# Three weight tiles of a decoder layer's mixer, laid 64 bytes lower in SBUF

## The chip, the cores and the metric

One core of a Trainium2 chip. The metric is the device time of one execution in microseconds (us), the median of the runs shown. The shorthand of the profile: PE is TensorE's matmul stream and PEld its weight loads, DVE is VectorE, ACT is ScalarE, POOL is GpSimd, SP is SyncE (here only a DMA queue).

## The reference, cut to what matters

One decoder layer on 512 tokens of width 1024, in float32: a half-step SwiGLU FFN, a mixer, and a second half-step FFN, each between a norm before and a norm after.

```
x = x + 0.5 * PostNorm_a(SwiGLU_1(PreNorm_a(x)))
x = x +       PostNorm_b(W_out [HGRN2_heads(h) ; mLSTM_heads(h)]),  h = PreNorm_b(x)
x = x + 0.5 * PostNorm_c(SwiGLU_2(PreNorm_c(x)))
```

All that matters here is the front of the mixer. It reads one combined projection of the normed input, cut into column groups of 512 (and a few gate columns):

```
hq, hf, hi, hgate, mq, mk, mv, mo, mig, mfg = split_cols(h @ w_in, SPLIT_SIZES)
forget = lbh + (1.0 - lbh) * sigmoid(hf)                     # HGRN2's forget gate
... silu(hq) ...                                             # HGRN2's queries
qk = silu(causal_depthwise_conv(concat([mq, mk]), conv_w, conv_b))   # mLSTM's q and k
```

Three of these groups, hf, hq and (mq, mk), are wanted with features on the partitions and tokens along the free axis; the others (hi, mv, hgate, mo) with tokens on the partitions.

## The kernel before, in words

**Numbers.** Every float32 matrix is split into a high part (ACT casts it to fp32r, line 283) and a low part (DVE subtracts the high one from the raw values, line 285). A product is three fp32r matmuls: high by high, high by low, low by high. A weight tile holds both parts one behind the other: 2 x 1024 floats for each partition, 8 KB.

**The weights' ring.** All weight tiles lie in one long SBUF tile, `w` (line 270): 96 floats of room in front, four places of 2048 floats, 128 floats of room behind. `split` (line 260) takes the next tile of a list made beforehand, asks `lie` (line 248) for a free place and a shift within it, and issues the cast and the subtraction. `LIES` (line 98) gives the shifts in floats for each kind of tile. For a tile that isn't "out" and isn't a 512-wide mixer tile (kind "any") it is 0 in all cases that matter here. The 512-wide tiles of the mixer (kind "mix") lie 16 floats (64 bytes) lower.

**The three projections.** Each of hf, hq and (mq, mk) has four weight tiles of 128 columns (`f` in `mix_items`), split and used in this order, and they take the places 0, 1, 3, 2 of the ring. The tile is the stationary operand, the transposed activations are the moving one: four tiles `xq0` to `xq3`, each of half of the features and half of the tokens (256), high and low part one behind the other.
- hf goes first. `head_mm` (line 543, matmuls on line 548) does the first 256 tokens while the first FFN's last rows are still being normed: 24 matmuls for a tile (8 slices of the features by 3 products). `forget_gates` then has `in_mm` do the other 256 tokens (`in_k`, line 534, matmuls on line 538): again 24 for a tile.
- hq and the convolution's (mq, mk) are jobs (`job_f`), 48 matmuls on line 538 for a tile, that the mixer's code pulls forward with `fill` between its own small matmuls. After the first (mq, mk) tile has begun come HGRN2's small matmuls (lines 1368, 1373, 1419), and after the fourth the gate rows (line 1466). After them come the token-major projections (lines 187 to 189, `mm3`), in which the 512-wide weight tile is the moving operand and the activations are the stationary one.

**The FFN products.** Line 608, in `prod`, is the FFNs' big group, with the same shape as lines 538 and 548: 128x128 weights and 256 moving columns, 24 matmuls for a product, 8 for each of the three pairs of parts. One layout detail is needed below. In the FFNs, tile `xq0` is viewed as `x0` (line 139), whose low part begins 16 floats (64 bytes) further on than in the other three. It is read by the middle eight matmuls of products p1, c1 and c3.

**Addresses in SBUF,** from the built program, in bytes within a partition: `w` begins at 87136, and its place 0 with the shift 0 at 87136 + 96 x 4 = 87520. `xq1`, `xq2`, `xq3`, `xq0` begin at 33440, 41632, 49824, 58016. Within a tile the slices of the features lie 512 bytes apart in the weights and 1024 bytes apart in the activations, and places lie 8192 bytes apart, so that start addresses modulo 512 stay the same through a tile.

Of the kernel before, what the change touches and what calls it, by code (L numbers as in the profile page):

```python
# [22 lines left out]
RAW, WBUF, PAD, LATE, NEXT, FRONT, STEP = 3, 4, 128, 112, 64, 96, 16  # L23
# [71 lines left out]

FREE = (2, 3, 0, 1)
FREE2 = (3, 2, 0, 1)
LIES = {"any": (0, -16, -80, 48), "mix": (-16, 0, -80, 48), "out": (-80, 48, 0, -16)}


class Load:
# [17 lines left out]
class Layer:  # L119
# [128 lines left out]
    def lie(self, kind):  # L248

        used = [o for _, o, _ in self.slot.values()]  # L250
        at = LIES[kind]

        first = 1 + (kind == "out")
        tries = [(n, d) for n in self.free for d in (at[:first] if n < 2 else at[first - 1 :: -1])]
        for n, d in tries + [(n, d) for d in at[first:] for n in self.free]:
            o = FRONT + 2 * D * n + d
            if o + 2 * D <= self.wt.shape[1] and all(abs(o - a) >= 2 * D for a in used):
                return n, o

    def split(self):  # L260

        nc = self.nc
        it = self.items.popleft()
        raw = self.raw[it.key]
        _, a, b = raw.shape
        if it.dst:
            w = it.dst()
        else:
            if self.wt is None:
                self.wt = self.wp.tile([P, 2 * D * WBUF + FRONT + PAD], F32R, name="w")  # L270
            if not self.slot and it.key[0] != "mix":
                self.free = deque(FREE2 if it.key[0] == "f2" else FREE)
            n, o = self.lie("out" if it.key[1] == "out" else "mix" if it.key[0] == "mix" and b == 512 else "any")
            self.free.remove(n)
            w = self.wt[:, o : o + 2 * D].rearrange("p (b k t) -> p b k t", b=2, k=a)
            self.slot[id(w)] = n, o, w
        hi, lo = self.both(w)
        if it.sums:
            raw, hi, lo = (self.flat(v)[:, QUARTER:] for v in (raw, hi, lo))
        self.ready.append((w, it.dst is not None))  # L280
        rows = it.rows
        if rows is None:
            nc.scalar.copy(hi, raw)  # L283
            yield
            self.low = nc.vector.tensor_tensor(lo, raw, hi.bitcast(F32), op=ALU.subtract)  # L285
        else:
            for j in range(a):
                nc.scalar.activation(hi[:, j], raw[:, j], AF.Copy, scale=rows[:, j : j + 1])
            yield
            for j in range(a):  # L290
                nc.vector.scalar_tensor_tensor(
                    lo[:, j], raw[:, j], rows[:, j : j + 1], hi[:, j].bitcast(F32), op0=ALU.mult, op1=ALU.subtract
                )
        with self.behind(*self.hold):
            for out, other in it.adds:
                o, c = self.raw[out], self.raw[other]

                late = out[1] >= (HEAD if out[0] == "f1" else 1)
                added = (nc.vector if late else nc.gpsimd).tensor_tensor(o, o, c, op=ALU.add)  # L299
                if not late:  # L300
                    self.pooled = added
        self.load_due(self.done)
        self.done += 1
        yield
# [410 lines left out]
    def start(self, norm, xn):  # L715
# [8 lines left out]
        split = self.split()  # L724
        step(q[1][0], q[1][1])
        next(split)
        step(q[1][0])
        next(split)
        step(q[0][0], q[1][0])
        head = deque(HEADS)  # L730
# [1170 lines left out]
```

## Time and profile before

| what | value |
|---|---|
| runs, us | 934.08, 934.02, 931.58; median 934.02 |
| the profiled execution's own time, us | 933.69 |
| its span on the core, us | 932.0 (1.69 lie around it) |
| granted TensorE clock | 0.998 of full speed |
| busy share of the span | PE 99%, DVE 82%, ACT 56%, POOL 20% |
| stages in the span, us | first FFN 0 to 342; hf, hq and convolution's projections with HGRN2's first matmuls 342 to 424; rest of the mixer to 603; second FFN to the end |

How to read it: the profile has a row for each group of instructions, with its count, its busy time and the mean length of one. A matmul's length is from its start to its modelled end, and matmuls are pipelined, so lengths overlap. What a stream of them costs is the pitch, the time from one start to the next. Where a row tells of one unbroken stretch, the pitch is its length less one matmul, over its count less one.

### The profile page before, as it was taken

To read this page: it belongs to the slowest core of one execution; us is meant where nothing else is said; L and a number is where in the kernel's file an instruction comes from. 1 tells how busy PE (TensorE), PEld (TensorE's weight loads), DVE (VectorE), ACT (ScalarE), POOL (GpSimd) and SP (SyncE) were. 2 spreads that over 40 slices of the span, in tenths; PEclk is the share of its full clock that TensorE was granted. 3 is DMA by queue.
4 is the path that set the end of the run, shared out by engine and by line. 5 is a ranking of instruction groups with operands and counts; after the bars stand their busy time and mean duration, and the time that the engine had idled before them with its cause. 6 is when DMAs were issued, how large, how long until landed. Compare 5 with 4: busy or idle time off the path is not lost.

```text
span 932.0 us, 18308 instructions
## 1 busy us (share of the span) xinstructions
PE 921.7 (99%) x7423; PEld 887.4 (95%) x7423; DVE 765.9 (82%) x992; ACT 525.2 (56%) x757; POOL 186.9 (20%) x256
## 2 busy tenths in 40 slices
PE   8999999999999999999999999999999999999997
PEld 7999999999999999998887888899999999999997
DVE  5899978889888776698847564799898989998886
ACT  6645455557565466956633444495454545756661
POOL 3531112121111045452321210304000000011002
PEclk9999999999999999999999999999999999999999
DMA  9245679776797925798742124452453435279542
GB/s 310 76 138 157 181 182 214 195 157 142 209 273 238 262 65 150 151 184 208 152 98 69 46 72 132 137 162 66 135 159 123 136 111 174 84 221 261 165 153 91
DMA packets 118766, 145.42 MB, mean 156 GB/s; under 512 B 7413, under 2 KB 91417, under 8 KB 118682
## 3 DMA queue, kind: packets, MB, share of 16 engines
q1 hardware_dynamic: 102714, 129.05, 44.2%
q0 software_dynamic: 15680, 14.69, 11.6%
q8 instruction: 58, 0.95, 0.4%
q10 hardware_dynamic: 288, 0.52, 0.2%
q14 instruction: 26, 0.21, 0.1%
HBM read 142.14 MB, written 31.46 MB: 186 GB/s over the span
## 4 chain that ended last, share of the span: by engine, by line
PE 62%; ACT 1%; DVE 0%; issue 0%; POOL 0%; DVEq 0%; POOLq 0%; ACTq 0%
PE ps L608 22%; PE ps L955 8%; PE ps L538 6%; PE ps L187 5%; PE ps L189 5%; PE ps L188 5%; PE ps L947 4%; PE ps L1373 2%; PE ps L353 1%; PE ps L548 1%; PE ps L1466 0%; PE ps L1671 0%; PE ps L1644 0%; PE ps L1419 0%; PE ps L1668 0%; PE ps L1431 0%
## 5 line engine op out<-in xcount | busy, mean ns | idle before, releaser
L283 ACT CAST w<-raw 128x1024 fp32r<-128x1024 f32 x246 | 251.3, 1028 | 199.0 <-PE ps L608 93.6
L285 DVE TENSOR_TENSOR w<-raw,w 128x1024 fp32r<-128x1024 f32 x246 | 298.9, 1219 | 30.9 <-ACT w L283 29.5
L608 PE MATMUL ps<-xq,w 128*128 128x256 f32 x2016 | 237.1, 277 | 0.0
L608 PEld LDWEIGHTS ps<-xq,w 128*128 128x128 f32 x2016 | 232.9, 188 | 0.0
L608 PE MATMUL ps<-sq,w 128*128 128x256 f32 x1512 | 178.0, 276 | 0.3
L608 PEld LDWEIGHTS ps<-sq,w 128*128 128x128 f32 x1512 | 174.2, 188 | 1.0 <-ACT ps L659 0.9
L299 DVE TENSOR_TENSOR raw<-raw,raw 128x1024 f32<-128x1024 f32 x72 | 89.8, 1251 | 7.8 <-DMA raw<-in_ffn_w_in_dram 6.1
L955 PE MATMUL ps<-w,hs 128*128 128x256 f32 x672 | 81.0, 276 | 0.0
L947 PE MATMUL ps<-w,hs 128*128 128x256 f32 x672 | 79.2, 276 | 0.0
L955 PEld LDWEIGHTS ps<-w,hs 128*128 128x128 f32 x672 | 78.4, 188 | 0.0
L187 PE MATMUL ps<-w,xq 128*128 128x512 f32 x192 | 77.9, 407 | 0.1
L947 PEld LDWEIGHTS ps<-w,hs 128*128 128x128 f32 x672 | 77.5, 188 | 0.0
L189 PE MATMUL ps<-w,xq 128*128 128x512 f32 x192 | 74.8, 391 | 0.0
L188 PE MATMUL ps<-w,xq 128*128 128x512 f32 x192 | 74.8, 390 | 0.0
L538 PE MATMUL ps<-xq,w 128*128 128x256 f32 x480 | 57.5, 282 | 0.0
L538 PEld LDWEIGHTS ps<-xq,w 128*128 128x128 f32 x480 | 56.6, 189 | 0.5 <-issue 0.5
L887 POOL DMA_DIRECT2D f2sums<-in_ffn_w_out_dram x15 | 20.0, 1482 | 176.9 <-DMA f2sums<-in_ffn_w_out_dram 176.9
L827 ACT CAST hs<-hf 128x1024 fp32r<-128x1024 f32 x32 | 33.7, 1053 | 28.8 <-PE ps L955 21.1
L828 DVE TENSOR_TENSOR hs<-hf,hs 128x1024 fp32r<-128x1024 f32 x32 | 39.1, 1221 | 8.7 <-ACT hs L827 8.2
L887 POOL DMA_DIRECT2D f1sums<-f1sums x26 | 23.2, 892 | 105.9 <-DMA f1sums<-in_ffn_w_out_dram 53.0
L187 PEld LDWEIGHTS ps<-w,xq 128*128 128x128 f32 x192 | 36.1, 188 | 8.5 <-issue 1.0
L189 PEld LDWEIGHTS ps<-w,xq 128*128 128x128 f32 x192 | 36.1, 188 | 8.1 <-DVE xq L360 0.3
(262 smaller groups left out, 1223.3 us busy)
## 6 DMA issues: line engine op xcount, KB each, us to landing
raw<-in_ffn_w_in_dram SPq DMA_DIRECT2D x98, 512.0 KB, 5.3
raw<-in_ffn_w_out_dram SPq DMA_DIRECT2D x44, 512.0 KB, 4.5
raw<-in_w_mix_in_dram SPq DMA_DIRECT2D x28, 512.0 KB, 3.6
raw<-f2sums SPq DMA_DIRECT2D x15, 512.0 KB, 5.6
raw<-f1sums SPq DMA_DIRECT2D x13, 512.0 KB, 7.6
raw<-in_w_mix_out_dram SPq DMA_DIRECT2D x8, 512.0 KB, 3.7
f2sums<-in_ffn_w_out_dram SPq DMA_DIRECT2D x30, 128.0 KB, 5.9
f2sums<-in_ffn_w_out_dram SPq DMA_DIRECT2D x15, 256.0 KB, 5.7
```

Of the source, the lines that this page charges most:

```text
L187: mm(ps, sh, mh, start=start, stop=False, **kw)
L188: mm(ps, sh, ml, start=False, stop=False, **kw)
L189: mm(ps, sl, mh, start=False, stop=stop, **kw)
L283: nc.scalar.copy(hi, raw)
L285: self.low = nc.vector.tensor_tensor(lo, raw, hi.bitcast(F32), op=ALU.subtract)
L299: added = (nc.vector if late else nc.gpsimd).tensor_tensor(o, o, c, op=ALU.add)
L538: mm(ps[:, u0:u1], w[:, a, k, :], self.xop(k, b, u0, u1), start=k + n + m == 0, stop=k == ND - 1 and n == 2, skip_group_check=True,)
L608: self.nc.tensor.matmul(ps[:, c], wb[b][:, k, v], left[d][:, k, :], start=first and a + n + k == 0, stop=n == 2 and k == KH - 1, skip_grou ...
L828: self.nc.vector.tensor_tensor(lo, src, hi.bitcast(F32), op=ALU.subtract)
L887: nc.gpsimd.dma_start(to[:, a:b], v, accum_op=ALU.add)
L947: mm(out, a[kk][:, i * P : (i + 1) * P], w[:, b, kk, QUARTER * v : QUARTER * (v + 1)], start=begin and c == kk == n == 0, stop=kk == 1 and ...
L955: mm(ps[:, QUARTER * c : QUARTER * (c + 1)], A[a][:, c], B[b], start=begin and c == n == 0, stop=n == 2, skip_group_check=True,)
```

## The change

`lie` gets a kind "low", that returns place 0 and a shift of -16 floats, with no search. `split` asks for it for a mixer tile that isn't 512 wide, whenever place 0 is free. With the order of places above, this holds for the first tile of each of the three projections, and for no other tile.

```
-LIES = {"any": (0, -16, -80, 48), "mix": (-16, 0, -80, 48), "out": (-80, 48, 0, -16)}
+LIES = {"any": (0, -16, -80, 48), "mix": (-16, 0, -80, 48), "low": (-16,), "out": (-80, 48, 0, -16)}
...
         first = 1 + (kind == "out")
+        if kind == "low":
+            return 0, FRONT + at[0]
         tries = [(n, d) for n in self.free for d in (at[:first] if n < 2 else at[first - 1 :: -1])]
...
-            n, o = self.lie("out" if it.key[1] == "out" else "mix" if it.key[0] == "mix" and b == 512 else "any")
+            mix = "mix" if b == 512 else "low" if 0 in self.free else "any"
+            n, o = self.lie("out" if it.key[1] == "out" else mix if it.key[0] == "mix" else "any")
```

In the built program three tiles begin at float 80 of `w` in place of float 96. With them the addresses of 150 instructions differ: three casts on ACT, three subtractions on DVE, and 144 matmuls (24 + 24 of hf, 48 of hq, 48 of mq). The order of the instructions on every engine, their shapes, their waits and all DMAs are the same as before.

## The prediction

> **What bounds the kernel now.** I read the page's busy times first, then its chain of work, then the stage that the change touches, by windows.
>
> ```profile
> PE 921.7 (99%) x7423; PEld 887.4 (95%) x7423; DVE 765.9 (82%) x992; ACT 525.2 (56%) x757; POOL 186.9 (20%) x256
> PE 62%; ACT 1%; DVE 0%; issue 0%; POOL 0%; DVEq 0%; POOLq 0%; ACTq 0%
> L608 PE MATMUL ps<-xq,w 128*128 128x256 f32 x2016 | 237.1, 277 | 0.0
> L538 PE MATMUL ps<-xq,w 128*128 128x256 f32 x480 | 57.5, 282 | 0.0
> ```
> ```profile
> 356.00:367.00 11.00, 11.00 (x95) 11.00 (x95) 6.26 (x8) 7.18 (x8) 8.24 (x16) 1.00 0.41 104
> 367.00:390.00 23.00, 23.00 (x198) 23.00 (x197) 15.29 (x27) 22.77 (x26) 12.76 (x22) 1.00 0.55 117
> 390.00:418.00 28.00, 28.00 (x250) 27.52 (x249) 24.96 (x35) 17.53 (x24) 14.51 (x16) 1.00 1.03 198
> ```
>
> PE is busy 99% of the span and makes nearly all of the chain. In the three windows, which hold hf's second half, hq and the convolution's projections (columns: the stretch, its length, then busy time of PE, PEld, DVE, ACT, POOL), PE is busy in every one of the 62 us. So the time here is the sum of the matmuls' pitches, and an edit pays only if it changes a pitch.
>
> The two group rows hold the clue: the same shape of matmul is 277 ns long on line 608 and 282 on line 538. So I read single stretches. The next rows are of the timeline (start, length, group, count); the first is an FFN stretch, the others the mixer's.
>
> ```profile
> 54.73 13.76 PE L608 MATMUL ps<-sq,w 128*128 128x256 f32 x120
> 355.60 34.09 PE L538 MATMUL ps<-xq,w 128*128 128x256 f32 x288
> 391.23 2.30 PE L538 MATMUL ps<-xq,w 128*128 128x256 f32 x18
> 393.82 15.40 PE L538 MATMUL ps<-xq,w 128*128 128x256 f32 x126
> 412.03 5.71 PE L538 MATMUL ps<-xq,w 128*128 128x256 f32 x48
> ```
>
> FFN: (13.76 - 0.28) / 119 = 113.3 ns a matmul. Mixer: (34.09 - 0.28) / 287 = 117.8 ns. So there are two rates, 4.5 ns apart, and the length of a matmul tells them apart: 276 ns at the fast one, 281 at the slow one. The next rows (count: shortest/median/longest length in ns, first and last start) show which stretch has which.
>
> ```profile
> L548 PE MATMUL ps<-xq,w x33: 276/276/276, 343.0 to 346.7; 128*128 128x256 f32 x33
> L548 PE MATMUL ps<-xq,w x24: 281/281/364, 352.7 to 355.5; 128*128 128x256 f32 x24
> L538 PE MATMUL ps<-xq,w x287: 281/281/281, 355.6 to 389.3; 128*128 128x256 f32 x144
> L538 PE MATMUL ps<-xq,w x17: 276/276/367, 391.2 to 393.1; 128*128 128x256 f32 x17
> L538 PE MATMUL ps<-xq,w x125: 281/281/681, 393.8 to 408.8; 128*128 128x256 f32 x125
> L538 PE MATMUL ps<-xq,w x45: 276/276/279, 412.3 to 417.3; 128*128 128x256 f32 x45
> ```
>
> The rate is not a property of a tile or a line: lines 538 and 548 have both, with operands at the same distances. It is a state. It holds without a single exception through 287 matmuls and changes at interruptions (at 391 and 412 small matmuls came between, and the stream came back fast). I take it for a phase between the weight loads and the moving reads.
>
> **The change part by part.** It adds, removes and reorders nothing. It makes the weights of three tiles begin 64 bytes lower. Take the distance from the moving operand's start to the weights' start, modulo 512 bytes. Everywhere on lines 538, 548 and 608 but in one place it is 480 - 160 = 320. In the three tiles it becomes 416 - 160 = 256.
>
> The one place is in the trace already: the middle third of products p1, c1 and c3 of line 608, whose activations lie 64 bytes higher: 480 - 224 = 256. So line 608 shows what eight matmuls at 256 do to the state. Three such products follow, each by the lengths before, within and after the eight (edges of a window take a neighbour or two with them):
>
> ```profile
> L608 PE MATMUL ps<-xq,w x6: 276/276/276, 626.7 to 627.3; 128*128 128x256 f32 x6
> L608 PE MATMUL ps<-xq,w x10: 274/280/282, 627.2 to 628.2; 128*128 128x256 f32 x10
> L608 PE MATMUL ps<-xq,w x15: 276/276/283, 628.5 to 630.1; 128*128 128x256 f32 x15
> ...
> L608 PE MATMUL ps<-xq,sq x8: 280/281/281, 602.6 to 603.5; 128*128 128x256 f32 x8
> L608 PE MATMUL ps<-xq,sq x10: 278/283/283, 603.4 to 604.4; 128*128 128x256 f32 x10
> L608 PE MATMUL ps<-xq,sq x7: 276/277/282, 604.7 to 605.4; 128*128 128x256 f32 x7
> ...
> L608 PE MATMUL ps<-xq,sq x8: 281/281/363, 606.3 to 607.2; 128*128 128x256 f32 x8
> L608 PE MATMUL ps<-xq,sq x10: 280/282/287, 607.1 to 608.1; 128*128 128x256 f32 x10
> L608 PE MATMUL ps<-xq,sq x6: 276/276/282, 608.5 to 609.1; 128*128 128x256 f32 x6
> ```
>
> Entered fast, the eight are somewhat slower and leave the stream fast. Entered slow (the other two, the only such ones), they are slower still, and leave it fast as well. So the stretch at 256 costs a little within and resets the state: whatever comes after it, at 320 again, is fast until something interrupts.
>
> *Gain: what comes after the moved tiles.* The row of 288 is hf's second half (4 tiles x 24) and hq (4 x 48). The moved tiles are 24 + 48 of it; the other 72 + 144 = 216 go from slow to fast. Of the convolution's first tile, 18 matmuls come before the interruption and 30 after it, so the row of 126 has 126 - 30 = 96 from the next two tiles. Together 312 x 4.5 ns = 1.40 us. The convolution's fourth tile is fast already, and line 548's second tile too.
>
> *Cost: the moved tiles themselves.* No row has more than eight in a row at 256; by medians these are 280 where they came in fast, 282 and 283 where slow. I take 282 for longer stretches, since it is between the three and both states lead there: 6 ns over fast, 1 over slow. Line 548's first tile, some 20 at 276: 0.12 us. hf's second half, 24 slow: 0.02. hq, 48 slow: 0.05. The convolution's, 18 fast and 30 slow: 0.14. The way out takes about three more at up to 283 (7 ns) four times: 0.08. Sum 0.41.
>
> *Bounds of that cost.* Above: all at 287, the longest seen, is 11 over fast and 6 over slow: 38 x 11 + 102 x 6 ns, or 1.03 us, plus the way out, 1.11. Below: they might settle at the fast length within a few, as the token-major matmuls do, whose distance is 256 as well (first stretch below early, second settled):
>
> ```profile
> L187 PE MATMUL ps<-w,xq x4: 393/398/477, 470.6 to 472.8; 128*128 128x512 f32 x4
> L187 PE MATMUL ps<-w,xq x22: 389/389/479, 537.8 to 552.1; 128*128 128x512 f32 x22
> ```
>
> Then 102 that are at 281 gain 4.5 ns each, 0.46 us, less the way out. So the sum is -1.40 + 0.41 = -0.99 us, between -0.3 (costly) and -1.8 (settling).
>
> *Nothing takes it back on another engine.* PE waits nowhere in the windows, and the splits are paced by PE, not the other way:
>
> ```profile
> L283 ACT CAST w<-raw x16: 1029/1046/1071, 341.1 to 417.5; 128x1024 fp32r<-128x1024 f32 x16
>   PE ps L538: 11.6, 4
> ```
>
> ACT's casts stood 11.6 us waiting for line 538 to free a place (the second row is of its idle time). The six moved split instructions write the same bytes at another address; at 1.05 us each beside a busy PE, even a tenth on each would stay under cover.
>
> **The rivals.**
> 1. *It does nothing:* where a weight tile lies beside the activations doesn't set the pitch, the rates and their changes on line 608 having another cause, such as the end of one pair of parts. Then every length stays and the time is 933.7. Against it: the pairs of parts change in the other products too, and in those 276 holds (the rows of line 608 differ from 276 only at the shifted eight). Chance 0.03.
>    The Trainium skill, "TensorE: Matmul & The Clock Gate", section "Step-by-step: what each phase is for", gives a reason for this rival: PE has two independent SBUF read ports, one for the moving operand and one for weight loads, so that loading the next weights takes no read bandwidth from the running matmul. By that rule the time stays 933.7; the trace disagrees so far, by the 4 to 7 ns between the shifted eight and their neighbours.
> 2. *It does nothing that lasts:* 256 resets the state only because the FFN returns to 320 after eight matmuls, at a certain phase; after 24 or 48 the stream comes out slow again. For it: no stretch that long is in the trace. Against it: the eight end in different phases (280, 282 and 283 medians) and all come out fast. Then the gain is gone. At the low end of the costs the time stays at 933.7. Chance 0.05.
> 3. *Slower:* as in 2, but with the costs paid (0.41), and the convolution's fourth tile, fast today after a stream that came in slow, comes back slow after HGRN2's small matmuls (48 x 4.5 = 0.22 us): +0.6, 934.3. This decides at one place, the first matmul after each moved tile: if lengths there are 281, it holds.
> 4. *Much slower:* the phase carries on into the token-major matmuls and they don't settle: 576 (three lines of 192) at 394 to 398 in place of 389, +2.9 us, with the costs 937.0. Against it: between lie the gate rows and small matmuls, and after each of many interruptions those lengths do settle.
> 5. *Much faster:* the moved tiles settle (-1.8), and the stream's state after interruptions turns for the better elsewhere: line 548's third and fourth tiles fast (48 x 4.5 = 0.2) and the token-major ones settled from their start (at 5 to 9 ns for some ten in each of a dozen stretches, an estimate from the two L187 rows, about 0.9): -2.9, 930.8.
>
> **How the numbers follow.** The profiled execution took 933.69 us (span 932.0 and 1.69 around it), 0.33 under the median 934.02; the sum puts it at 932.7, and the median at 933.0, which I predict. The lowest run, 931.58, lies 2.4 under the median, about what all the slow matmuls on lines 538 and 548 would save at the fast rate (some 500 x 4.5 ns = 2.2); I take it that runs differ by such luck. Chances: forecast 0.70, rivals 1 and 2 together 0.08, rival 3 0.07, rival 4 0.04, rival 5 0.11. The range holds the forecast with its bounds (-1.8 to -0.3, from either 933.69 or 934.02, so 931.9 to 933.7), rivals 1 and 2, part of rival 3, and below a median of lucky runs: 931.4 to 934.2. About 0.3% (2.8 us) is what a measurement can tell from no change. So the forecast and rivals 1 to 3 are "same", 0.85; rival 5 is faster, 0.11; rival 4 slower, 0.04.
>
> **What would show it.** Right: line 538 has 276 ns in hf's second to fourth tiles (from 358 us on), in hq's second to fourth and in the convolution's second and third, its group mean falls from 282 to about 279, the moved tiles show 280 to 283, and the stage from 342 to 424 is 1 us shorter with PE still busy throughout. Wrong: 281 right after a moved tile (rivals 1 to 3), or PE waiting in 356 to 418.

## The result and the profile after

The changed kernel takes 933.28 us (median of 22 runs, 931.47 to 934.73) beside 931.53 us for the kernel before (median of 22, 929.57 to 934.08): a ratio of 1.0019, 95% interval 1.0013 to 1.0026. So it is 0.19% slower, about 1.75 us, where the forecast said 1 us faster. That 933.28 lies close to the 933.0 of the forecast is luck: the start was put 2.5 us too high (934.02 for 931.53), the change 2.8 us too low, and the two nearly cancel. The profiled execution took 933.47 us, its span 931.8.

The page of the changed kernel (line numbers are 3 higher from line 250 on, so 608 is now 611, 538 is 541, 548 is 551):

```profile
PE 922.9 (99%) x7423; PEld 888.5 (95%) x7423; DVE 766.7 (82%) x992; ACT 525.2 (56%) x757; POOL 186.2 (20%) x256
...
PE 59%; DVE 2%; DMA 1%; issue 1%; ACT 1%; DVEq 0%; POOLq 0%; POOL 0%; ACTq 0%
...
L611 PE MATMUL ps<-xq,w 128*128 128x256 f32 x2016 | 237.1, 277 | 0.0
...
L541 PE MATMUL ps<-xq,w 128*128 128x256 f32 x480 | 57.8, 282 | 0.0
```

PE is as busy as before and the FFN's group is unchanged. Line 541 should have fallen to a mean of 279; it stays at 282. The windows that the prediction read (same columns), of the changed kernel:

```profile
356.00:367.00 11.00, 11.00 (x96) 11.00 (x95) 7.17 (x10) 8.90 (x10) 8.81 (x19) 1.00 0.44 107
367.00:390.00 23.00, 23.00 (x198) 23.00 (x197) 15.52 (x27) 22.78 (x26) 12.98 (x21) 1.00 0.62 123
390.00:418.00 28.00, 28.00 (x248) 27.52 (x247) 25.86 (x36) 17.21 (x24) 15.59 (x17) 1.00 1.00 195
```

PE never waits in these windows, so what counts is still the pitch. The timeline of the changed kernel (start, length, group, count), first the stage from its first matmul to the first token-major one, then three windows within it:

```profile
340.54 6.12 PE L551 MATMUL ps<-xq,w 128*128 128x256 f32 x48
...
353.81 34.24 PE L541 MATMUL ps<-xq,w 128*128 128x256 f32 x288
...
423.01 0.48 PE L187 MATMUL ps<-w,xq 128*128 128x512 f32 x1
...
353.81 2.80 PE L541 MATMUL ps<-xq,w 128*128 128x256 f32 x22
...
365.17 5.56 PE L541 MATMUL ps<-xq,w 128*128 128x256 f32 x45
...
371.04 16.65 PE L541 MATMUL ps<-xq,w 128*128 128x256 f32 x140
```

The row of 288 has become longer, 34.24 us for 34.09. The last three rows give pitches: (2.80 - 0.28) / 21 = 120.0 ns in hf's moved tile, (5.56 - 0.28) / 44 = 120.0 in hq's, and (16.65 - 0.28) / 139 = 117.8 in the three tiles behind hq's. So the moved tiles have a rate of their own, 120.0 ns. The lengths of single matmuls (count: shortest/median/longest, first and last start) tell it tile by tile; 283 ns goes with a pitch of 120.0, as 276 with 113.3 and 281 with 117.8:

```profile
L551 PE MATMUL ps<-xq,w x19: 278/283/386, 340.5 to 342.8; 128*128 128x256 f32 x19
L551 PE MATMUL ps<-xq,w x24: 276/276/367, 351.0 to 353.7; 128*128 128x256 f32 x24
L541 PE MATMUL ps<-xq,w x23: 283/283/283, 353.8 to 356.4; 128*128 128x256 f32 x23
L541 PE MATMUL ps<-xq,w x73: 281/281/283, 356.4 to 364.9; 128*128 128x256 f32 x73
L541 PE MATMUL ps<-xq,w x47: 281/283/283, 364.9 to 370.4; 128*128 128x256 f32 x47
L541 PE MATMUL ps<-xq,w x144: 281/281/281, 370.8 to 387.6; 128*128 128x256 f32 x144
L541 PE MATMUL ps<-xq,w x97: 279/281/281, 396.1 to 407.4; 128*128 128x256 f32 x97
```

Read the second to the fourth row: the stream is at 276 just ahead of hf's moved tile, is at 283 through it, and comes out at 281. Behind hq's moved tile (fifth and sixth row) and behind the convolution's (last row) it is at 281 as well. Nowhere does a moved tile leave the stream at 276. That is what the prediction named as the sign of rivals 1 to 3. The token-major matmuls and ACT's casts are as before, so neither rival 4 nor a lost cover plays a part:

```profile
L187 PE MATMUL ps<-w,xq x23: 389/389/479, 533.8 to 550.6; 128*128 128x512 f32 x23
...
L286 ACT CAST w<-raw x16: 1027/1045/1070, 339.4 to 416.0; 128x1024 fp32r<-128x1024 f32 x16
...
  PE ps L541: 11.5, 4
```

One thing doesn't fit yet. The profile of before had 281 in these tiles as well, so against it the stage (first matmul of line 551 to the first token-major one) costs hardly more: 423.01 - 340.54 = 82.47 us here, and 82.28 there. The experiments start from that.

### The profile page after: what moved, and what is told of

The parts are those of the page before. It is cut to its first block, busy times and chain, and to the rows that moved or that the text cites. A ratio compares the mean times of both kernels' runs of the same rounds, so it can differ in the third digit from the quotient of the medians.

```text
span 931.8 us, 18308 instructions
## 1 busy us (share of the span) xinstructions
PE 922.9 (99%) x7423; PEld 888.5 (95%) x7423; DVE 766.7 (82%) x992; ACT 525.2 (56%) x757; POOL 186.2 (20%) x256
## 4 chain that ended last, share of the span: by engine, by line
PE 59%; DVE 2%; DMA 1%; issue 1%; ACT 1%; DVEq 0%; POOLq 0%; POOL 0%; ACTq 0%
PE ps L611 19%; PE ps L958 8%; PE ps L541 6%; PE ps L187 5%; PE ps L189 5%; PE ps L188 5%; PE ps L950 4%; PE ps L1376 2%; PE ps L551 1%; DMA raw<-in_ffn_w_in_dram 1%; PE ps L356 1%; DVE w L288 1%; PE ps L1469 0%; PE ps L1674 0%; PE ps L1647 0%
## 5 line engine op out<-in xcount | busy, mean ns | idle before, releaser
L611 PE MATMUL ps<-xq,w 128*128 128x256 f32 x2016 | 237.1, 277 | 0.0
```

The lines of the kernel that those rows point to most:

```text
L611: self.nc.tensor.matmul(ps[:, c], wb[b][:, k, v], left[d][:, k, :], start=first and a + n + k == 0, stop=n == 2 and k == KH - 1, skip_grou ...
```

## The experiments

Two theories were to be told apart. **Count:** what follows a stretch at distance 256 depends on how many matmuls it has, eight in the FFN and 24 or 48 in the mixer. **Operand:** it depends on which operand makes the step back to 320, the activations in the FFN and the weights in the mixer. (Product c1 takes its pairs of parts in another order, by line 604, so there it is the last eight matmuls that read the shifted low part and not the middle ones; the activations step back all the same.) And a question came before both: how the kernel before usually runs. All ratios below are to the kernel before on the same chip. None of the kernels leaves out part of the computation.

### The kernel before again, and the changed one

No edit: `e1`, `e14` and `e15` are the kernel before, `e16` is the changed kernel.

> The kernel before, unchanged, for a second profile of it. Theory A: the first profile, with 117.8 ns a matmul from 347 to 409 us, showed what is not the usual case of this kernel; the usual one has 113.3 ns in most of hf, hq and the convolution's projections, so that this profile has fewer than the first one's 520 or so matmuls at 117.8 on lines 538 and 548 (down to 100), and line 538's group mean is 276 to 279 in place of 282. Theory B: the projections always run at 117.8 as in the first profile (mean 282), and the change lost its time elsewhere. Time ratio 1.000 either way.

> The kernel before, unchanged, a third profile. If 113.3 is the usual rate of hf's second half and hq, it is here too, and the stage from the first matmul on line 548 to the token-major projections takes 80.4 to 81 us (82.3 in the first profile, 80.4 in the second).

> The kernel before, unchanged, a fourth profile, with the same expectation as the third.

> The changed kernel, unchanged, for a second profile and beside the others on one chip. 120 in the moved tiles, 117.8 behind them again, the stage 82.3 to 82.5 us; ratio 1.002.

Lengths in hf's second half and hq, from the three new profiles of before, one after the other:

```profile
L538 PE MATMUL ps<-xq,w x288: 276/276/276, 353.4 to 385.9; 128*128 128x256 f32 x144
```
```profile
L538 PE MATMUL ps<-xq,w x295: 275/276/364, 353.9 to 389.0; 128*128 128x256 f32 x148
```
```profile
L538 PE MATMUL ps<-xq,w x293: 275/276/364, 354.1 to 389.0; 128*128 128x256 f32 x147
```

All three have 276 where the first profile had 281 without exception. More of the first of them, by its timeline and by the lengths in its convolution's tiles:

```profile
340.14 6.12 PE L548 MATMUL ps<-xq,w 128*128 128x256 f32 x48
...
353.42 32.80 PE L538 MATMUL ps<-xq,w 128*128 128x256 f32 x288
...
420.58 0.48 PE L187 MATMUL ps<-w,xq 128*128 128x512 f32 x1
```
```profile
L538 PE MATMUL ps<-xq,w x18: 280/281/364, 387.8 to 389.8; 128*128 128x256 f32 x18
...
L538 PE MATMUL ps<-xq,w x114: 276/276/282, 392.2 to 405.0; 128*128 128x256 f32 x114
```

The kernel before usually runs hf's second half and hq at 113.3 ns: (32.80 - 0.28) / 287. `e6` and `e10` below, which leave the mixer as it was, have 276 there too. The first profile parts from all others of this study in the last tile of hf's first half, which is at 281 there and at 276 in the others. The stage of `e1` is 420.58 - 340.14 = 80.44 us, and 80.44 and 80.45 in the other two; the profile that the prediction read had 82.28. The change takes 82.47 (82.47 again in `e16`), which is 2.03 more than usual. `e1`'s mean on line 538 is 277, as its first theory had it. `e1` came to 932.04 us, a ratio of 1.0008 (0.9999 to 1.0017) for unchanged code, so the timings can be off by about 0.1%; `e16` to 933.65 us, 1.0027 (1.0016 to 1.0037).

The first profile was unusual at its start, too. The timelines of the two kernels, before and then after:

```profile
9.79 1.97 PE L353 MATMUL ps<-ident,xn 128*128 128x128 f32 x8 [1.72 <-DVE xn L470]
```
```profile
8.07 1.97 PE L356 MATMUL ps<-ident,xn 128*128 128x128 f32 x8
...
770.91 2.97 PE L611 MATMUL ps<-sq,w 128*128 128x256 f32 x24 [0.45 <-DVE ps L630]
...
914.15 11.47 PE L950 MATMUL ps<-w,hs 128*128 128x256 f32 x96
```

Before waited 1.72 us here; the other three profiles of before began these matmuls at 7.93 us. The profile of after has mishaps of its own: a wait of 0.45 at 771 us, and its last 175 matmuls (the row is of the last 96) at a pitch of (11.47 - 0.28) / 95 = 117.8, 0.8 us in all. `e16` has the slow end too, no profile of before has it; but `e7` and `e9`, two executions of one kernel, differ in it, so whether it belongs to the change is open. With these mishaps on both sides the two spans, 932.0 and 931.8, differ by less than the change costs.

### One moved tile at a time

```
-            mix = "mix" if b == 512 else "low" if 0 in self.free else "any"
+            mix = "mix" if b == 512 else "low" if it.key[1] == 0 else "any"
```

The 0 is hf's tile (`e2`); it is 4 for hq's (`e3`) and 8 for the convolution's (`e4`).

> Only hf's first tile lies lower; hq's and the convolution's first tiles lie as before. Theory A (a moved tile settles at 120.0 ns a matmul and leaves the stream at 117.8 until something interrupts it): hf's second to fourth tiles and all of hq at 117.8, that is 72 + 192 matmuls x 4.5 ns = 1.2 us, and 48 in the moved tile at 6.7 over 113.3 = 0.3; up to +1.5 us or ratio 1.0016 against a kernel before at 113.3, and +0.2 us against one at 117.8. Theory B: ratio 1.000 and no 120 in hf's moved tile that before does not have.

> Only hq's first tile lies lower. Theory A: its 48 matmuls at 120.0 ns, hq's other 144 at 117.8 whatever hf's rate was: +0.3 + 0.65 = up to +1.0 us (1.0010) against a kernel before at 113.3. The interruption after hq (HGRN2's small matmuls) makes what follows as in before. Theory B: 1.000.

> Only the first tile of the convolution's projections lies lower. Theory A: its 48 matmuls at about 120, the next two tiles' 96 at 117.8, and that is what before's first profile had for 126 of these 144 already: +0.1 us if before is always so there, up to +0.75 (1.0008) if it is usually at 113.3. Theory B: 1.000.

With hf's tile alone, what comes behind it, to the end of hq:

```profile
L541 PE MATMUL ps<-xq,w x266: 281/281/284, 357.2 to 388.4; 128*128 128x256 f32 x133
```

With hq's alone, what comes behind it:

```profile
L541 PE MATMUL ps<-xq,w x149: 281/281/283, 371.0 to 388.5; 128*128 128x256 f32 x149
```

With the convolution's alone, hf and hq, and what comes behind its tile:

```profile
L541 PE MATMUL ps<-xq,w x288: 276/276/276, 353.8 to 386.3; 128*128 128x256 f32 x144
...
L541 PE MATMUL ps<-xq,w x99: 279/281/283, 394.4 to 406.0; 128*128 128x256 f32 x99
```

In each, 281 begins behind the moved tile, and the last two rows show 276 ahead of it. With hf's or hq's tile alone it also goes on into the convolution's tiles, across the small matmuls, where theory A expected them as in before. The convolution's first three tiles with hq's alone moved:

```profile
L541 PE MATMUL ps<-xq,w x144: 280/281/682, 390.9 to 408.6; 128*128 128x256 f32 x144
```

The stages are 82.31, 81.93 and 81.05 us, so 1.87, 1.49 and 0.61 over 80.44. At 6.7 ns for a matmul of a moved tile and 4.5 for one behind it that is otherwise at 276, the 126 of the convolution included, the sums are 1.92, 1.54 and 0.67. The times: 933.09 us, 1.0024 (1.0014 to 1.0033); 932.53, 1.0012 (1.0004 to 1.0021); 931.87, 1.0006 (0.9997 to 1.0014). They don't add up to the whole change, and shouldn't: a stream that hf's tile has brought to 117.8 can't be brought there by hq's again. Their order shows in the stages, of one profile each; the intervals of the three ratios overlap, and the last isn't clear of no change.

### Count or operand

`e5` gives the weights' step the FFN's count: only hf's tile is touched, its low part begins where the change puts the tile and its high part behind it, 16 floats further on than two parts end to end, so that in each half of the tokens 16 matmuls are at 320 and the last eight at 256. For that the second half goes one pair of parts after the other, as the first half and the FFN do.

```
+                w = self.wt[:, o : o + 2 * D + 32].rearrange("p (b x) -> p b x", b=2)[:, :, :D].rearrange("p b (k t) -> p b k t", k=a)
...
+            hi, lo = lo, hi
...
+                        ps[:, t0:t1], w[:, 1 - a, k, :], self.xop(k, b, t0, t1),
```

`e6` gives the activations' step the mixer's count: all of `x0` lies 64 bytes higher, not only its low part, so that 24 or 48 matmuls in a row are at 256.

```
-        x0 = self.xt[0].rearrange("p (b x) -> p b x", b=2)[:, :, :D].rearrange("p b (k t) -> p b k t", k=KH)
+        x0 = self.xt[0][:, STEP : STEP + 2 * D].rearrange("p (b k t) -> p b k t", b=2, k=KH)
```

> Only in hf's first tile, and only its low part, lies 64 bytes lower (it stands ahead of the high part, which keeps its distance of 320), and the tile's second 256 tokens go product by product, so that twice there is a stretch of eight matmuls at distance 256, made by the weights' address, as long as the FFN's that the activations' address makes. Theory L (length decides: eight don't settle at 120, so the stream comes out at 113.3; 24 settle and come out at 117.8): hf's second to fourth tiles and hq at 113.3, ratio 1.000. Theory O (the operand decides: when the weights' address goes back the stream comes out at 117.8, when the activations' does, at 113.3): the stream comes out of the eight at 117.8, 72 + 192 matmuls x 4.5 ns = +1.2 us, 1.0013.

> The kernel before, but both parts of the FFN's view of the first activation tile begin 64 bytes on, not the low part alone: products p1, c1 and c3 of line 608 have all their 24 matmuls at distance 256, made by the activations' address. Theory L: they settle at 120 and leave the stream at 117.8, where it stays to the next such product: nearly all of line 608's 3700 matmuls 4.5 ns longer, +15 us, its group mean 281. Theory O: it comes out at 113.3 after each; the cost is 16 more matmuls at some 6 ns in each of about 20 products, +2 us.

Eight by the weights (line 543 has the tile in the second half of the tokens, line 555 what follows):

```profile
L543 PE MATMUL ps<-xq,w x24: 276/276/283, 354.5 to 357.1; 128*128 128x256 f32 x24
...
L555 PE MATMUL ps<-xq,w x264: 281/281/284, 357.2 to 388.2; 128*128 128x256 f32 x132
```

Twenty-four by the activations, entered at 276 and, further down, at 281 (before, within, behind):

```profile
L608 PE MATMUL ps<-sq,w x20: 276/276/277, 69.8 to 72.0; 128*128 128x256 f32 x20
...
L608 PE MATMUL ps<-xq,w x21: 279/283/287, 72.8 to 75.2; 128*128 128x256 f32 x21
...
L608 PE MATMUL ps<-xq,w x25: 276/276/279, 75.2 to 77.9; 128*128 128x256 f32 x25
...
L608 PE MATMUL ps<-xq,w x48: 281/281/363, 610.4 to 616.1; 128*128 128x256 f32 x48
...
L608 PE MATMUL ps<-xq,w x19: 283/283/286, 617.0 to 619.2; 128*128 128x256 f32 x19
...
L608 PE MATMUL ps<-xq,w x47: 276/276/283, 619.2 to 624.4; 128*128 128x256 f32 x47
```

Count falls: eight by the weights come out at 281, 264 matmuls long, and 24 or 48 by the activations come out at 276, in all 18 stretches that run straight on at 320. (Two more, at the start of the second FFN, end at other matmuls; 281 follows the second of them, the row of 48 above.) Both settle at 283 within. Of the two theories, operand stands. `e5` took 933.31 us, 1.0025 (1.0015 to 1.0035): eight matmuls in each half of one tile cost about as much as the whole change, more than the 1.0013 expected, since here too the convolution's tiles stay at 281. Its stage is 82.20 us, 1.76 over 80.44. `e6`, a single run of 932.22, can't be told from no change; its first FFN, from its first product to hf's first matmul, takes 329.42 us beside 328.15 to 328.30 in the four profiles of before.

### Other distances

`e7` and `e9` are one kernel, timed in `e9`: the three tiles lie 128 bytes lower than the others, a distance of 192. `e8`: 384 lower (-96 floats in the line below), 448.

```
-LIES = {"any": (0, -16, -80, 48), "mix": (-16, 0, -80, 48), "low": (-16,), "out": (-80, 48, 0, -16)}
+LIES = {"any": (0, -16, -80, 48), "mix": (-16, 0, -80, 48), "low": (-32,), "out": (-80, 48, 0, -16)}
```

`e10` moves the low part of the FFN's `x0` by 128 bytes in place of 64 (192 by the activations), `e11` does that and `e9`'s edit. `e12` takes the kernel before and moves the third tile of each projection 64 bytes up, to 384.

```
-        x0 = self.xt[0].rearrange("p (b x) -> p b x", b=2)[:, :, :D].rearrange("p b (k t) -> p b k t", k=KH)
+        x0 = tuple(self.xt[0][:, o : o + D].rearrange("p (k t) -> p k t", k=KH) for o in (0, D + 2 * STEP))
```
```
+            if it.key[0] == "mix" and b != 512 and n == 3:
+                o += 16
```

> The changed kernel with the three tiles 128 bytes lower in place of 64: distance 192. If the distance of 256 is what is bad, another one gives another settled pitch in the moved tiles; if any departure from 320 is, it gives 120 and leaves the stream at 117.8 as 64 bytes do, and the stage from 342 to 424 us in the first profile is as long as in the changed kernel (82.5 us).

> The changed kernel with the three tiles 384 bytes lower: distance 448. As the one with 128 bytes: 120 in the moved tiles and 117.8 behind them if any departure from 320 does it, another pitch if the distance itself matters.

> The kernel with the three tiles 128 bytes lower again, now timed. Its first profile had no pitch but 113.3 and 117.8 in the moved tiles, and the stream went from 117.8 to 113.3 right behind hf's and the convolution's. Theory O2 (at distance 192 the stream keeps the rate that it has, and the weights' return to 320 sets it to 113.3): the loss of the changed kernel is gone, ratio to the kernel before 0.9985 to 1.000, as many of before's executions have 113.3 there anyway. If 1.002 as for 64 bytes, the moved tiles' pitch isn't the cause.

> The kernel before with the low part of the FFN's view of the first activation tile 128 bytes on in place of 64: the middle eight matmuls of p1, c1 and c3 are at distance 192 in place of 256, by the activations' address. The mixer's tiles lie as before. If 192 costs nothing by the activations either, some 23 stretches that cost about 0.05 us each (eight at 282 and three at the way out, against 276) save 1.2 us, 0.9988. If their return from 192 doesn't set the rate as the one from 256 does, the second FFN, which starts at 117.8 (its first matmuls at 602.6 in the first profile), stays there: up to 2000 x 4.5 ns, +9 us, 1.009.

> Both: the three mixer tiles 128 bytes lower and the FFN's low part 128 bytes on. If both theories hold, 0.998 to 0.999 (1.2 us of the FFNs, up to 1 us of the mixer); if e10 stays at 117.8 in the second FFN, this does too.

> The kernel before with the third tile of each of the three projections (place 3) 64 bytes higher in place of the first tile 64 bytes lower: distance 384. If going 64 bytes off either way settles at 120 and the weights' return leaves 117.8, hf's and hq's fourth tiles are at 117.8 after it; if only the lower side does, they keep the rate from before the moved tile or get 113.3.

In `e9`, 26 matmuls of the convolution's moved tile, and its last three with what comes behind it:

```profile
L541 PE MATMUL ps<-xq,w x26: 278/279/680, 390.8 to 394.2; 128*128 128x256 f32 x26
...
L541 PE MATMUL ps<-xq,w x99: 276/276/285, 394.4 to 405.6; 128*128 128x256 f32 x99
```

Within the tile the starts stand 117.8 ns apart (the mean of 23 steps from 391.5 to 394.3 us), though the lengths are 279 at this distance. Set the second row beside that of the convolution's tile alone at 256, above: the same 99 matmuls, at 276 here and at 281 there. This tile's address differs by 64 bytes, and hf's second half and hq are at 276 ahead of it in both. At 192 a tile of weights keeps the rate that it comes in with, 113.3 or 117.8, and 113.3 follows; so it is at 448. Neither of the outcomes set down for `e7` and `e8` came. The stage is 80.58 us in `e7` and `e9` and 80.55 in `e8`. `e9` took 930.82 us, 0.9997 (0.9987 to 1.0008); `e7` and `e8`, a single run each, 930.56 and 931.33.

`e10` is the largest miss of the study, far above all that was expected of it: 951.05 us, 1.0205 (1.0183 to 1.0226). Its page; then line 608 behind one of the shifted stretches; then a stretch that is entered at 276, ahead of it, within it and behind it (the middle row takes a neighbour with it):

```profile
L608 PE MATMUL ps<-xq,w 128*128 128x256 f32 x2016 | 244.2, 281 | 0.0
L608 PE MATMUL ps<-sq,w 128*128 128x256 f32 x1512 | 183.9, 281 | 0.4 <-ACT w L283 0.2
L955 PE MATMUL ps<-w,hs 128*128 128x256 f32 x672 | 84.1, 281 | 0.0
L947 PE MATMUL ps<-w,hs 128*128 128x256 f32 x672 | 82.0, 281 | 0.0
```
```profile
L608 PE MATMUL ps<-xq,w x87: 280/281/281, 75.7 to 94.3; 128*128 128x256 f32 x87
...
L608 PE MATMUL ps<-xq,w x8: 276/276/276, 705.0 to 705.8; 128*128 128x256 f32 x8
...
L608 PE MATMUL ps<-xq,w x9: 279/279/280, 705.9 to 706.8; 128*128 128x256 f32 x9
...
L608 PE MATMUL ps<-xq,w x8: 280/281/281, 706.8 to 707.7; 128*128 128x256 f32 x8
```

Both FFNs run at 281 nearly from end to end; some 440 of their 5700 matmuls of this shape are at 276 or 277, most of them behind interruptions, until the next shifted stretch. The group of 2016 goes from 237.1 to 244.2 us of busy time. Some 4872 matmuls (2016 + 1512 + 672 + 672) at 4.5 ns would be 21.9 us; the medians differ by 19.8. Read the last three rows: the length of 279 goes with 117.8 ns at this distance, as in `e9`, and from the first of these eight on the starts are 117 to 119 ns apart. So it is the step to 192 that brings 117.8 here, and the step back leaves it as it is. It is so in all ten stretches of `e10` and `e11` that are entered at 276. By the weights it was otherwise: the step to 192 left hf's and hq's moved tiles at 276, and the step back from a tile at 117.8 brought 113.3. The operand matters at 192 as well, in another way than at 256. (One stretch is different in both runs, the first of the second FFN: it is entered at 281 and left at 276, before other matmuls interrupt it.) `e11`, 950.1 us, 1.0206 (1.0192 to 1.0220), is the same with the mixer's stage at 80.54. `e12` has a pattern of lengths at 384, with a mean pitch of 118.2 to 118.6, and behind hf's and hq's the stream is at 113.3 at once; but it came in at 113.3 too, so whether the return sets the rate isn't shown there. Its single run took 930.50.

### Keeping what works

`e13` has no step in the activations at all. In the FFNs too it is now the weights that step, 128 bytes lower, in place 0.

```
-        self.xh = [x0, *self.xq[1:]]
+        self.xh = self.xq
...
+            if n == 0 and it.key[1] != "out" and b != 512:
+                o -= 32
```

> The kernel before without the 64 bytes in the FFN's view of the first activation tile (so no stretch at 256 is left in the FFNs), and with every tile of 128 or 256 columns that takes place 0 lying 128 bytes lower, in the FFNs and in the mixer. If weights that return from 192 set the stream to 113.3 and 192 itself costs nothing, all of line 608 is at 113.3 without the 23 stretches of about 0.05 us: -1.2 us, and the mixer's projections at 113.3 behind each first tile, up to -0.5: 0.998 to 0.999. If it doesn't hold in the FFNs, the second one stays at 117.8 as in e10: 1.008 or more.

Lengths on the first FFN's line 610 (608 in before), and hf's second half with hq:

```profile
L610 PE MATMUL ps<-xq,w x864: 276/276/387, 47.1 to 232.1; 128*128 128x256 f32 x173
```
```profile
L540 PE MATMUL ps<-xq,w x288: 276/276/276, 353.0 to 385.5; 128*128 128x256 f32 x144
```

From 48 to 332 us the first FFN runs unbroken at 113.3, without the stretches at 120. From its first product to hf's first matmul it takes 327.53 us, beside 328.15 to 328.30 in the four profiles of before. The mixer's stage, at 80.55, gains nothing on the usual 80.44. In all `e13` takes 929.90 us, 0.9991 (0.9982 to 0.9999): the lowest median here, below both kernels, by about as much as the unchanged kernel was off in `e1`, so the gain itself is likely rather than settled.

### What the distances do, together

| distance | within | behind it, returned by the weights | returned by the activations |
|---|---|---|---|
| 320 | 113.3 or 117.8, as it came | | |
| 256 | settles at 120.0 | 117.8 (the change, e2 to e5, e16) | 113.3 (before, e6) |
| 192 | by the weights 113.3 or 117.8, as it came; by the activations 117.8, however it came (e10, e11) | 113.3 (e7, e9, e11, e13) | 117.8, as within (e10, e11; one stretch of each 113.3) |
| 448 | 113.3 or 117.8, as it came | 113.3 (e8) | not tried |
| 384 | a pattern, 118.2 to 118.6 | 113.3, but it came in at 113.3 (e12) | not tried |

## Why the prediction was wrong, point by point

**The bound was right.** PE's pitch sets this stage from 356 to 418 us, nothing waits there, and nothing on another engine took anything back. That there are two rates 4.5 ns apart, that they last until something disturbs them, and that addresses disturb them, was right too.

**The step that failed:** "the stretch at 256 costs a little within and resets the state: whatever comes after it, at 320 again, is fast until something interrupts". The rows of line 608 showed that for one operand only: in all of them the activations step away and back. The weights' step back leads to the other rate: 281, not 276, right behind every moved tile. The text spoke of the distance as if only the difference of the two addresses counted; `e5` (281 behind eight by the weights) and `e6` (276 behind 24 by the activations) show that this isn't so. The gain of 312 x 4.5 = 1.40 us is thus a loss of that size against the usual run of the kernel before.

**The start was unusual.** The forecast took "fast" for something to be gained, since the one profile had 117.8 in hf's second half, hq and two tiles of the convolution. Three later profiles have 113.3 there. Had the step held, the change would have had next to nothing to gain from that start. The hint was in the text, that the lowest run lies 2.4 us under the median and that "runs differ by such luck"; it was used for the range and not for the forecast. The medians of 22 runs say the same: before came to 931.53, not 934.02.

**The cost of the moved tiles** (0.41) had the right sign, and its length of 282 was one short of the 283 measured. But it was counted over 281 for most of them. Against 276 it is larger: hf's 24 and hq's 48 cost 72 x 6.7 = 0.48 us, the convolution's 30 later ones 0.20, its first 18, at 281 without the change, 18 x 2.2 = 0.04. With 312 x 4.5 = 1.40 behind them that makes 2.1 us, beside 2.03 measured in the stage and 1.75 in the medians. hf's first half, priced at 0.12, cost nothing: its first two tiles take 6.12 us with the moved tile at 283 (the row at 340.54 above) and without it in `e1` (the row at 340.14).

**The rivals.** The sign of rival 3, 281 right after a moved tile, came true in every place. Its reason, the length of the stretch, fell in `e5` and `e6`; its extra price, the convolution's fourth tile at 281, didn't come; and its time, 934.3, was worked out from the same unusual start. Rival 1 fell: at the same order of instructions, an address alone moves the pitch from 113.3 to 120.0. (What the prediction said against it was not quite so: line 608 differs from 276 elsewhere too, with 24 matmuls at 281 from 23.2 to 26.0 us in the first profile, behind an interruption.) The Trainium skill, "TensorE: Matmul & The Clock Gate", section "Step-by-step: what each phase is for", has weight loads take no read bandwidth from a running matmul. By the prediction's use of that rule the pitch should not have moved; it moved by up to 6.7 ns in 113.3. That the two reads get in each other's way is not shown by this, for no run looked at the reads themselves.

**What stays open.** Why the operand matters, and why 192 differs from 256, was not tried at the level of the reads themselves. A rival is untested: in every step back from 256 the weights went up in address and the activations down, so which operand stepped and which way it stepped can't be told apart there. Nor is it settled what decides at interruptions. In all ten profiles in which the convolution's first tile lies as before, what follows the two 512-wide matmuls within that tile has the rate that hq ended with: 276 in six (`e1`, `e6`, `e10`, `e12`, `e14`, `e15`), 281 in four (the first profile, `e2`, `e3`, `e5`). Yet the tile's first 18 matmuls, ahead of them, are at 281 in nine of the ten and at 276 in the first profile. So an interruption doesn't simply end a rate; how it comes back isn't shown.

## What to carry to other kernels

Where a stream of matmuls with a weight load each is the bound, its pitch may depend on where the two operands start in SBUF relative to each other, and on what came before; read it as (stretch - one length) / (count - 1), and try the addresses. A precedent in the trace holds for a new case only if the same thing moves: here the distance was the same, and the operand and the direction of its step weren't. And when one profile shows a rate that can flip, take more profiles before counting on it as the start.

## What was not expected of the hardware

A matmul of 128x256 with its weight load has three lasting pitches here, 113.3, 117.8 and 120.0 ns, at a granted clock of 0.998 to 0.999 in every profile; which it has depends on start addresses 64 bytes apart, and at a distance of 320, or of 192 and 448 made by the weights, on its history. A step of 128 bytes in one operand, for eight matmuls at a time, made the whole kernel about 2% slower (`e10`, 1.0205), since a step like the one at 705.9 us left the stream at 117.8 for the matmuls that followed.
